# A two-layer encoder in split float32: six weight tiles between the layers get their low parts by accumulating DMA instead of GpSimd subtraction

## The chip, the cores and the metric

The kernel runs on one core of a Trainium2 chip. The metric is the device time of one execution in microseconds (us). The core's engines are named as the profile names them: PE is TensorE's matmul, PEld its weight load, DVE is VectorE, ACT is ScalarE, POOL is GpSimd, SP is SyncE. Engines run in parallel, each its own instructions in order, and wait for one another by semaphores. DMA transfers are issued by the queues of SP, ACT and POOL and run on 16 DMA engines.

## The reference

Two layers (`DEPTH = 2`) work on a float32 stream of 512 tokens by 1024 channels. Each is:

```
h    = rms_norm(x, g_pre_mix);  proj = h @ w_in          # 1024 x 5632
o_a, o_b, o_m = 2-D neighbourhood attention (6 heads, bias from a table rpb_na),
                dilated windows with ALiBi (6 heads), cross-attention to 256 memory tokens
merged = sum of sigmoid(gates) * (o @ w_br)               # three branches
x = x + rms_norm(merged @ w_out, g_post_mix)
u = depthwise_conv(rms_norm(x, g_pre_ffn) @ w_up);  a, b = split(u)
x = x + rms_norm((gelu(a) * b) @ w_down, g_post_ffn)
```

The memory tokens' keys and values are `rms_norm(mem) @ w_mem_kv`, with weights of their own in each layer. The output is `x` after the second layer.

## The kernel before, in words

**Split operands.** All is held transposed: channels on the 128 partitions, tokens along the free axis. Each float32 operand of a matmul is split in two: a high part `hi` in the matmul's own format (float32r) and a low part `lo`, the source less `hi`. A product is three matmuls (`mm3`): hi by hi, hi by lo, and last the weight's `lo` by the other side's `hi`.

**Weights.** `weights` (L227) brings one weight tile of 1024 x 128 (512 KB) by SP's queue into a raw buffer `wraw`, of which there are three. With a `slot` given, it is then split in two chunks of 128 partitions x 512 numbers, each into a buffer of the pool `m` (32 buffers). `split` (L223) copies a chunk to `hi` on ACT, and forms `lo` as `wraw - hi` on VectorE or on GpSimd, as its last argument says. Both read `wraw`, and SP loads the next tile into it when both are done.

**Between the layers.** At the end of layer 0 the new `x` comes in two halves of 256 tokens. For each, a chain on VectorE and ACT normalises and adds (`y<-y,pt`, `x<-x,y`) and sums squares (`acc<-acc,sq`); PE turns the sum into a column (`pt<-mean,acc`), ACT and DVE make the root's reciprocal. Beside this chain PE runs work of layer 1 in an order laid down when the program is built (a planner with a clock of estimated costs, class `Woven`; it is the same order on PE before and after the change):

- `mem_kv`: four tiles of `w_mem_kv`, called kv0 to kv3 here, by the normalised memory tokens.
- `run_group`, first half of tokens: six tiles of `w_in`, called gw0 to gw5, in pairs. A pair takes turns over the eight 128-row pieces k = 0 to 7 of the weights; pieces 0 to 3 lie in a tile's first chunk, 4 to 7 in its second. Pair gw0, gw1 goes into two `mm` banks, pair gw2, gw3 into `o` and `pt`, pair gw4, gw5 into two `s` banks.
- `run_group`, second half, by the not yet normalised `ka` tiles of `raw_end_job`; then a factor `R` scales it, which the second chain yields.

**Who splits which tile.** The strings `KVE` (L38) and `GEN` (L38) say it by one letter for each tile: V is VectorE, G is GpSimd. G has kv2, kv3, gw0, gw1, gw3 and gw5: six tiles, twelve chunks. Their `lo` are first read by PE's third matmul for piece 0 or 4.

**What else POOL does there.** It copies halves of memory keys, and builds layer 1's bias tiles in `a_bias` (L593): a transfer of the table (`y<-in_rpb_dram`, 128 KB, on POOL's queue) into a buffer `y` that the second chain's `x<-x,y` must have read, then three subtractions `y<-mask,y`.

Of the kernel before, what the change touches and what calls it, by code (L numbers as in the profile page):

```python
# [10 lines left out]
ALU = mybir.AluOpType  # L11
# [9 lines left out]
KD = D_MODEL // 128  # L21
# [6 lines left out]
FIRST = (0, 3, 4, 7, 6, 1)  # L28
# [6 lines left out]

LAT_QK, LAT_SM, LAT_T, LAT_V, LAT_T2 = 1.0, 4.5, 1.5, 2.0, 0.6
STEP_A, STEP_B, STEP_M = 9.0, 9.0, 5.5
SQG, LOG, GEN, KVE = {0: (), 1: ()}, {0: (), 1: ()}, 'GGVGVG', 'VVGG'  # L38
SD1 = 4.0
MARGIN = 0.3  # L40
SB = True
# [1 line left out]
KVD, GWD, NG, LAT1 = 7.3, 1.0, 2, 12.0  # L43
# [76 lines left out]
def tile_hybrid_encoder(ctx, tc, xT, memT, memg, vecs, rpb, w_in, w_kv, w_bra, w_brb, w_brm,  # L120
                        w_out, w_up, w_down, c_ident, c_mask, c_tab0, c_tab1, out):
    nc = tc.nc
# [13 lines left out]
    uid, last_copy, last_act, crit, last_lo = [0], [None], [None], [None], {}  # L136
    wv = Woven(tc)

    def nm(s):
        uid[0] += 1  # L140
        return f"{s}_{uid[0]}"


    def big(dt=F32R, shape=(128, 512)):
        return mp.tile(list(shape), dt, tag="m", name=nm("m"))
# [28 lines left out]
    def f32(ap):  # L174
        return ap.bitcast(F32)

    G = nc.gpsimd
    ACT, V = Counted(nc.scalar, wv, 0.1, 0.8e-3), Counted(nc.vector, wv, 0.065, 1.05e-3)

    DUP, MDUP = G, G  # L180
    MSQ = G

    def ready(least):
# [34 lines left out]
    def behind(ins, other):  # L218

        if other is not None and ins is not other:  # L220
            tc.add_manual_dep(ins, other.name, ORDER, reason="issue order")

    def split(src, hi, lo, eng=None):  # L223
        last_copy[0] = ACT.copy(hi, src).ins
        last_lo[eng or V] = (eng or V).tensor_sub(lo, src, f32(hi)).ins

    def weights(src, K, C, slot=None, eng=None, after=None):  # L227

        raw = wp.tile([128, K, C], F32, tag="wraw", name=nm("wraw"))
        nc.sync.dma_start(out=raw, in_=src)  # L230
        if slot is None:
            hi = wp.tile([128, K, C], F32R, tag="whi", name=nm("whi"), bufs=2)
            lo = wp.tile([128, K, C], F32R, tag="wlo", name=nm("wlo"), bufs=2)
            split(raw, hi, lo, eng)
            behind(last_copy[0], after)
            return [(hi[:, k, :], lo[:, k, :]) for k in range(K)]
        n = 512 // C
        w = []
        for k in range(0, K, n):
            c = min(n, K - k)  # L240
            hi, lo = slot(F32R, (128, c, C)), slot(F32R, (128, c, C))
            split(raw[:, k:k + c, :], hi, lo, eng)
            w += [(hi[:, i, :], lo[:, i, :]) for i in range(c)]
        return w

# [68 lines left out]
    def sumsq_add(acc, src, first, slot=None, eng=None):  # L314
        if first:
            ACT.activation(acc, src, AF.Square)
        else:
            n = acc.shape[-1]
            sq = slot((128, 256)) if slot else small("sq2", 4) if n == 256 else small("sq", 1, (128, 512))
            ACT.activation(sq, src, AF.Square)  # L320
            (eng or V).tensor_add(acc, acc, sq)
# [34 lines left out]
    def rtile():  # L356
        return tp.tile([128, 512], F32, tag="R", name=nm("R"), bufs=1)
# [6 lines left out]
    def pre_norm_job(l, goff, acc, hs, i):  # L364
        half, box = HALVES[i], []
        yield from rstd_job(acc if isinstance(acc, list) else [acc[:, half]], 256, box)
        for k in range(KD):
            g = g0[:, k:k + 1] if l == 0 and goff == V_PRE else vec[:, l, goff + k:goff + k + 1]
            normed(xh(k, half), g, box[0], hs[k][0][:, half], hs[k][1][:, half],
                   G if k in LOG[l > 0 and goff == V_PRE] else V)  # L370
        crit[0] = last_copy[0]
        yield 1.2
        wv.give(f"h{l}.{goff}.{i}")
# [73 lines left out]
    def h_tiles():  # L447
        return [(htile(), htile()) for _ in range(KD)]


    def mem_norm_job(l, hm, slot):
        raws = []
        for k2 in range(KD // 2):
            t = slot(F32, (128, 2, N_MEM))
            nc.scalar.dma_start(out=t, in_=memT[:, 2 * k2:2 * k2 + 2, :])
            raws += [t[:, 0, :], t[:, 1, :]]
        acc = small("h32", 3)
        for k in range(KD):
            sumsq_add(acc, raws[k], k == 0, None, MSQ if l else V)
        yield 14.0  # L460
        box = []
        yield from rstd_job([acc], N_MEM, box)
        for k in range(KD):
            t = slot(F32R, (128, 2, N_MEM))
            normed(raws[k], mg[:, k:k + 1], box[0], t[:, 0, :], t[:, 1, :])
            hm.append((t[:, 0, :], t[:, 1, :]))
        yield 1.2
        wv.give(f"mem{l}")
# [10 lines left out]
    def mem_kv(l, hm, km, vm, pre=()):  # L479
        wv.need(f"mem{l}")  # L480
        for m in range(4):
            w = pre[m] if pre else weights(w_kv[l, m], KD, 128)
            ps = mmbank((128, N_MEM))
            linear(ps, w, hm, slice(0, N_MEM))
            if m < 2:
                t, u = big(F32R, (128, 2, N_MEM)), big(F32R, (128, 2, N_MEM))
                twice_split(ps, (t[:, 0, :], t[:, 1, :]), (u[:, 0, :], u[:, 1, :]), None, MDUP)
                km.append((t, u))
            else:
                vT = big(F32, (128, 256))  # L490
                ACT.copy(vT, ps)
                wv.spawn(mem_v_job(l, vT, vm))


    def group_weights(srcs, engs):
        return [weights(s, KD, 128, big, e) for s, e in zip(srcs, engs)]
# [19 lines left out]
    def proj(l, m, hs, after=None):  # L516
        w = weights(w_in[l, m], KD, 128, after=after)
        ps = mmbank()
        linear(ps, w, hs)
        return ps  # L520
# [366 lines left out]
    gw = group_weights([w_in[0, m] for m in FIRST[:2]], (V, V))  # L887
# [14 lines left out]
    for l in range(depth):  # L902
# [41 lines left out]
        for m in range(KD):  # L944
# [3 lines left out]
            hi, lo = big(), big()  # L948
# [4 lines left out]
        hs, R, gw = h_tiles(), rtile(), []  # L953
# [44 lines left out]
        if l == depth - 1:  # L998
            sublayer_end(l, V_POSTF, w_of, fs, 2, None)
            while wv.jobs:  # L1000
                wv._step()
        else:
            hm, km, vm = [], [], []
            wv.spawn(mem_norm_job(l + 1, hm, htile), 20.0)
            pre, R, raw, box = [], rtile(), [], []

            def then(a, i, l=l, box=box):
                box.extend(h_tiles())
                return pre_norm_job(l + 1, V_PRE, a, box, i)

            gw = []

            def kv_ahead(l=l, pre=pre, gw=gw):
                pre.append(weights(w_kv[l + 1, 0], KD, 128, htile))
                yield KVD
                for i in (1, 2, 3):
                    yield 0.9
                    pre.append(weights(w_kv[l + 1, i], KD, 128, big, G if KVE[i] == 'G' else V))
                wv.give(f"kv{l + 1}")
                for m in range(NG):  # L1020
                    yield GWD
                    gw.extend(group_weights([w_in[l + 1, FIRST[m]]], [G if GEN[m] == 'G' else V]))
                wv.give(f"gw{l + 1}")

            sublayer_end(l, V_POSTF, w_of, fs, 1, [then, (box, raw, R)], (1.4, LAT1), lambda: wv.spawn(kv_ahead()))
            wv.need(f"kv{l + 1}")
            mem_kv(l + 1, hm, km, vm, pre)
            wv.need(f"gw{l + 1}")
            gw += group_weights([w_in[l + 1, m] for m in FIRST[NG:]], [G if e == 'G' else V for e in GEN[NG:]])
            wv.need(f"h{l + 1}.{V_PRE}.0")  # L1030
            hs = box

# [92 lines left out]
```

## Time and profile before

| | us |
|---|---|
| median of 3 runs | 1551.7 |
| the three runs | 1549.61, 1551.7, 2167.76 |
| profiled execution | 1551.73 |
| its span, first to last instruction | 1550.0 |
| PE busy | 1522.5 (98%) |
| DVE busy | 951.6 (61%) |
| ACT busy | 712.7 (46%) |
| POOL busy | 149.7 (10%), 217 instructions |

The profiled execution's time is its span and 1.73 us around it. The busy shares are means over the whole span; the change touches some 50 us of it, about 766 to 815 us from its start, and that stretch is to be read by itself.

### The profile page before, as it was taken

What the parts mean: (1) busy time and instruction counts of PE and PEld (TensorE: products, weight loads), DVE (VectorE), ACT (ScalarE), POOL (GpSimd) and SP (SyncE); (2) the same over time, 40 slices, a digit from 0 to 9 for tenths busy, and PEclk for the clock granted to TensorE, in tenths of its full rate; (3) what the DMA queues carried; (4) which work ended last, traced back from release to release, by engine and by line L of the source; (5) the groups of instructions that cost most, each with busy time, mean ns of one, the idle gap of its engine ahead of it and who ended that gap; (6) DMA issues with size and microseconds to landing.
All of it is one profiled execution on the core that took longest, in us unless ns stands there. A gap on an engine that the chain in (4) does not pass through costs nothing.

```text
span 1550.0 us, 20648 instructions
## 1 busy us (share of the span) xinstructions
PE 1522.5 (98%) x7970; PEld 1300.1 (84%) x7970; DVE 951.6 (61%) x1684; ACT 712.7 (46%) x1266; POOL 149.7 (10%) x217
## 2 busy tenths in 40 slices
PE   8999999999999999999989999999999999999997
PEld 7988888888988888888888888888889888888887
DVE  6685676335777777742497756753456977776233
ACT  5565554336544444532355555532354544444231
POOL 3340000110000000000154300002100000000000
PEclk9999999999999999999999999999999999999999
DMA  7221213235113322333431221132350233323331
GB/s 246 89 88 64 62 57 107 84 95 165 53 59 100 100 96 95 118 90 101 129 102 59 78 66 58 61 104 88 102 177 15 82 96 99 101 99 89 99 105 63
DMA packets 45810, 144.91 MB, mean 93 GB/s; under 512 B 5376, under 2 KB 9600, under 8 KB 45712
## 3 DMA queue, kind: packets, MB, share of 16 engines
q1 hardware_dynamic: 43776, 139.85, 28.5%
q10 hardware_dynamic: 1296, 2.10, 0.4%
q0 software_dynamic: 640, 1.64, 0.3%
q8 instruction: 62, 1.02, 0.3%
q14 instruction: 36, 0.29, 0.1%
HBM read 141.48 MB, written 2.10 MB: 93 GB/s over the span
## 4 chain that ended last, share of the span: by engine, by line
PE 91%; DVE 6%; ACT 2%; issue 1%; DMA 0%; SPq 0%; ACTq 0%; DVEq 0%
PE mm L247 80%; PE s L247 4%; PE o L247 3%; PE pt L258 2%; DVE m L114 1%; DVE y L114 1%; PE pt L247 1%; DVE ka L114 1%; DVE x L114 1%; ACT y L114 1%; DVE st L114 0%; DVE acc L114 0%; DMA x<-in_xT_dram 0%; DVE wlo L114 0%; ACT whi L114 0%
## 5 line engine op out<-in xcount | busy, mean ns | idle before, releaser
L247 PE MATMUL mm<-h,whi 128*128 128x512 f32 x2496 | 776.5, 392 | 0.0
L247 PEld LDWEIGHTS mm<-h,whi 128*128 128x128 f32 x2496 | 462.0, 188 | 91.3
L247 PE MATMUL mm<-h,wlo 128*128 128x512 f32 x1248 | 486.9, 390 | 0.0
L114 DVE TENSOR_TENSOR wlo<-wraw,whi 128x1024 fp32r<-128x1024 f32 (+1 forms) x213 | 259.2, 1217 | 284.7 <-ACT whi L114 282.3
L114 ACT CAST whi<-wraw 128x1024 fp32r<-128x1024 f32 (+1 forms) x213 | 221.4, 1040 | 307.8 <-PE mm L247 293.4
L247 PEld LDWEIGHTS mm<-h,wlo 128*128 128x128 f32 x1248 | 234.5, 188 | 49.6
L247 PE MATMUL mm<-m,whi 128*128 128x512 f32 (+1 forms) x800 | 215.1, 356 | 1.0 <-DVE m L114 0.8
L247 PEld LDWEIGHTS mm<-m,whi 128*128 128x128 f32 x800 | 141.8, 189 | 22.8 <-PE mm L247 1.3
L247 PE MATMUL mm<-m,wlo 128*128 128x512 f32 (+1 forms) x400 | 142.1, 355 | 0.0
L114 DVE SCALAR_TENSOR_TENSOR y<-y,vec,y 128x511 f32<-128x511 f32 x176 | 130.5, 748 | 3.5 <-ACT y L114 0.9
L114 DVE TENSOR_TENSOR y<-mm,R 128x512 f32<-128x512 f32 x82 | 56.4, 688 | 68.5 <-PE mm L247 68.5
L247 PEld LDWEIGHTS mm<-m,wlo 128*128 128x128 f32 x400 | 75.5, 189 | 10.9
L802 POOL TENSOR_TENSOR m<-m,y 128x512 f32<-128x512 f32 x28 | 36.1, 1289 | 399.4 <-DVE y L114 399.4
L114 ACT ACTIVATE y<-y,vec 128x512 f32<-128x512 f32 x88 | 71.1, 815 | 2.3 <-DVE y L114 1.9
L247 PE MATMUL mm<-m,m 128*128 128x512 f32 x240 | 63.5, 394 | 0.0
L114 ACT ACTIVATE y<-y 128x512 f32<-128x512 f32 x44 | 27.9, 633 | 71.7 <-DVE y L114 71.3
L114 ACT CAST m<-pt 128x512 fp32r<-128x512 f32 (+1 forms) x72 | 38.6, 541 | 46.8 <-PE pt L258 38.5
L114 ACT ACTIVATE y<-y,st 128x256 f32<-128x256 f32 (+1 forms) x80 | 43.8, 549 | 30.4 <-DVE st L114 28.9
L114 DVE TENSOR_TENSOR acc<-acc,sq 128x256 f32<-128x256 f32 (+1 forms) x80 | 41.1, 514 | 26.6 <-ACT sq L114 24.7
L114 DVE TENSOR_TENSOR m<-pt,m 128x512 fp32r<-128x512 f32 (+1 forms) x72 | 45.1, 630 | 19.9 <-ACT m L114 18.6
L114 ACT CAST m<-y 128x512 fp32r<-128x512 f32 x32 | 19.9, 622 | 72.5 <-DVE y L114 72.5
L247 PE MATMUL mm<-h,m 128*128 128x256 f32 x312 | 49.1, 301 | 2.0 <-ACT h L114 1.0
(154 smaller groups left out, 1789.9 us busy)
## 6 DMA issues: line engine op xcount, KB each, us to landing
wraw<-in_w_in_dram SPq DMA_DIRECT2D x88, 512.0 KB, 3.7
wraw<-in_w_up_dram SPq DMA_DIRECT2D x88, 512.0 KB, 3.6
wraw<-in_w_down_dram SPq DMA_DIRECT2D x32, 512.0 KB, 3.5
wraw<-in_w_out_dram SPq DMA_DIRECT2D x16, 512.0 KB, 3.9
wraw<-in_w_down_dram SPq DMA_DIRECT2D x16, 384.0 KB, 3.1
wraw<-in_w_kv_dram SPq DMA_DIRECT2D x8, 512.0 KB, 4.0
wraw<-in_w_bra_dram SPq DMA_DIRECT2D x16, 192.0 KB, 2.3
x<-in_xT_dram SPq DMA_DIRECT2D x8, 256.0 KB, 7.3
```

The source lines that it names most:

```text
L114: return op(*args, **kw)
L247: wv.pe(nc.tensor.matmul(ps, a, b, start=first, stop=last), cost)
L258: wv.pe(nc.tensor.transpose(ps[:, 128 * i:128 * i + 128], s, ident), 0.11)
L802: (V if br == 2 and m >= 6 else G).tensor_add(acc[m], acc[m], gs)
```

## The change

In six tiles the letter G becomes D. For a D tile ACT still copies the chunk to `hi`. GpSimd then writes `-hi` into `lo`, one instruction with one input, and issues a DMA that reads the same chunk of the weights from memory once more and adds it onto `lo` where it lies. `lo` is again the weight less `hi`. `wraw` is now read by ACT alone. The two G tiles of layer 0's first group stay as they were.

```diff
--- before.py
+++ after.py
@@ -35,7 +35,7 @@
 
 LAT_QK, LAT_SM, LAT_T, LAT_V, LAT_T2 = 1.0, 4.5, 1.5, 2.0, 0.6
 STEP_A, STEP_B, STEP_M = 9.0, 9.0, 5.5
-SQG, LOG, GEN, KVE = {0: (), 1: ()}, {0: (), 1: ()}, 'GGVGVG', 'VVGG'
+SQG, LOG, GEN, KVE = {0: (), 1: ()}, {0: (), 1: ()}, 'DDVDVD', 'VVDD'
 SD1 = 4.0
 MARGIN = 0.3
 SB = True
@@ -178,6 +178,7 @@
     ACT, V = Counted(nc.scalar, wv, 0.1, 0.8e-3), Counted(nc.vector, wv, 0.065, 1.05e-3)
 
     DUP, MDUP = G, G
+    ENG = {'G': G, 'V': V, 'D': 'D'}
     MSQ = G
 
     def ready(least):
@@ -239,7 +240,12 @@
         for k in range(0, K, n):
             c = min(n, K - k)
             hi, lo = slot(F32R, (128, c, C)), slot(F32R, (128, c, C))
-            split(raw[:, k:k + c, :], hi, lo, eng)
+            if eng == "D":
+                last_copy[0] = ACT.copy(hi, raw[:, k:k + c, :]).ins
+                nc.gpsimd.tensor_scalar_mul(lo, f32(hi), -1.0)
+                nc.gpsimd.dma_start(out=lo, in_=src[:, k:k + c, :], accum_op=ALU.add)
+            else:
+                split(raw[:, k:k + c, :], hi, lo, eng)
             w += [(hi[:, i, :], lo[:, i, :]) for i in range(c)]
         return w
 
@@ -1015,18 +1021,18 @@
                 yield KVD
                 for i in (1, 2, 3):
                     yield 0.9
-                    pre.append(weights(w_kv[l + 1, i], KD, 128, big, G if KVE[i] == 'G' else V))
+                    pre.append(weights(w_kv[l + 1, i], KD, 128, big, ENG[KVE[i]]))
                 wv.give(f"kv{l + 1}")
                 for m in range(NG):
                     yield GWD
-                    gw.extend(group_weights([w_in[l + 1, FIRST[m]]], [G if GEN[m] == 'G' else V]))
+                    gw.extend(group_weights([w_in[l + 1, FIRST[m]]], [ENG[GEN[m]]]))
                 wv.give(f"gw{l + 1}")
 
             sublayer_end(l, V_POSTF, w_of, fs, 1, [then, (box, raw, R)], (1.4, LAT1), lambda: wv.spawn(kv_ahead()))
             wv.need(f"kv{l + 1}")
             mem_kv(l + 1, hm, km, vm, pre)
             wv.need(f"gw{l + 1}")
-            gw += group_weights([w_in[l + 1, m] for m in FIRST[NG:]], [G if e == 'G' else V for e in GEN[NG:]])
+            gw += group_weights([w_in[l + 1, m] for m in FIRST[NG:]], [ENG[e] for e in GEN[NG:]])
             wv.need(f"h{l + 1}.{V_PRE}.0")
             hs = box
```

The scheduler that lays out each engine's instructions moves some of them. On POOL, from the second of the two places where its D chunks stand (gw3 and gw5; `m` are the `lo` and `hi` chunks, `in_rpb_dram` the bias table), before:

```order
L225 TENSOR_TENSOR m_7245<-wraw_7242,m_7244 128x512
L225 TENSOR_TENSOR m_7249<-wraw_7242,m_7248 128x512
L225 TENSOR_TENSOR m_7265<-wraw_7262,m_7264 128x512
L225 TENSOR_TENSOR m_7269<-wraw_7262,m_7268 128x512
L596 DMA y_7760<-in_rpb_dram 128x256
L599 TENSOR_TENSOR y_7759<-mask,y_7760 128x256 x2
L599 TENSOR_TENSOR y_7760<-mask,y_7760 128x256
```

and now:

```order
L245 TENSOR_SCALAR m_7253<-m_7252 128x512
L246 DMA m_7253<-in_w_in_dram 128x512
L245 TENSOR_SCALAR m_7258<-m_7257 128x512
L602 DMA y_7772<-in_rpb_dram 128x256
L246 DMA m_7258<-in_w_in_dram 128x512
L245 TENSOR_SCALAR m_7275<-m_7274 128x512
L605 TENSOR_TENSOR y_7771<-mask,y_7772 128x256
L246 DMA m_7275<-in_w_in_dram 128x512
L245 TENSOR_SCALAR m_7280<-m_7279 128x512
L605 TENSOR_TENSOR y_7771<-mask,y_7772 128x256
L246 DMA m_7280<-in_w_in_dram 128x512
L605 TENSOR_TENSOR y_7772<-mask,y_7772 128x256
```

The table's transfer and two of the three subtractions that wait for its landing now stand between the weights' own transfers. At the first place (kv2, kv3, gw0, gw1) eight subtractions become eight pairs of `TENSOR_SCALAR` and `DMA`, with nothing between them.

On VectorE, at the start of the second chain (`wraw` and `m` are gw4's chunks, whose `lo` VectorE forms; `y` and `x` are the chain), before:

```order
L114 TENSOR_TENSOR y_6072<-y_6072,pt_7304 128x256
L114 TENSOR_TENSOR y_6073<-y_6073,pt_7304 128x256
L114 TENSOR_TENSOR m_7255<-wraw_7252,m_7254 128x512
L114 TENSOR_TENSOR x<-x,y_6072 128x256
L114 TENSOR_TENSOR m_7259<-wraw_7252,m_7258 128x512
L114 TENSOR_TENSOR x<-x,y_6073 128x256
L114 SCALAR_TENSOR_TENSOR ka_7296<-x,vec,ka_7296 128x256
L114 TENSOR_TENSOR y_6074<-y_6074,pt_7304 128x256
```

and now:

```order
L114 TENSOR_TENSOR y_6072<-y_6072,pt_7316 128x256
L114 TENSOR_TENSOR y_6073<-y_6073,pt_7316 128x256
L114 TENSOR_TENSOR x<-x,y_6072 128x256
L114 TENSOR_TENSOR x<-x,y_6073 128x256
L114 TENSOR_TENSOR y_6074<-y_6074,pt_7316 128x256
L114 TENSOR_TENSOR m_7265<-wraw_7262,m_7264 128x512
L114 SCALAR_TENSOR_TENSOR ka_7308<-x,vec,ka_7308 128x256
L114 TENSOR_TENSOR m_7269<-wraw_7262,m_7268 128x512
L114 SCALAR_TENSOR_TENSOR ka_7309<-x,vec,ka_7309 128x256
```

Both of gw4's subtractions now come behind the first two additions to `x`.

## Rows read from the trace of the kernel before

**Rows 1.** Page, chain that ended last: shares of the span by engine.

```profile
PE 91%; DVE 6%; ACT 2%; issue 1%; DMA 0%; SPq 0%; ACTq 0%; DVEq 0%
```

**Rows 2.** Timeline of TensorE, 740 to 830 us: start, duration, instruction, count [idle before <-releaser].

```profile
783.59 0.58 PE L247 MATMUL pt<-mean,acc 128*128 128x1 f32 x4 [3.46 <-DVE acc L114]
...
786.10 4.79 PE L247 MATMUL mm<-h,m 128*128 128x256 f32 x30
...
795.72 3.12 PE L247 MATMUL mm<-h,m 128*128 128x256 f32 x24
...
799.04 0.52 PE L247 MATMUL pt<-h,m 128*128 128x256 f32 x3
...
804.44 5.92 PE L247 MATMUL s<-h,m 128*128 128x256 f32 x48
...
813.64 0.58 PE L247 MATMUL pt<-mean,acc 128*128 128x1 f32 x4 [1.16 <-DVE acc L114]
```

**Rows 3.** Stretches: length, busy time of PE, PEld, DVE, ACT, POOL, PEclk, DMA, GB/s.

```profile
785.00:788.00 3.00, 2.90 (x15) 2.61 (x14) 2.57 (x8) 1.44 (x5) 2.13 (x6) 0.50 0.03 5
790.00:794.00 4.00, 4.00 (x36) 4.00 (x35) 3.73 (x11) 2.98 (x9) 0.00 (x0) 1.00 0.00 0
```

**Rows 4.** Timeline of GpSimd (POOL), 700 to 920 us.

```profile
768.30 6.93 POOL L225 TENSOR_TENSOR m<-wraw,m 128x512 fp32r<-128x512 f32 x5 [105.56 <-ACT m L114]
776.61 4.24 POOL L225 TENSOR_TENSOR m<-wraw,m 128x512 fp32r<-128x512 f32 x3 [1.39 <-ACT m L114]
...
795.61 2.99 POOL L225 TENSOR_TENSOR m<-wraw,m 128x512 fp32r<-128x512 f32 x2 [8.35 <-PE s L258]
800.96 2.92 POOL L225 TENSOR_TENSOR m<-wraw,m 128x512 fp32r<-128x512 f32 x2 [2.36 <-ACT m L114]
```

**Rows 5.** Groups on POOL, 700 to 920 us: count, busy us, mean ns.

```profile
L225 POOL TENSOR_TENSOR m<-wraw,m 128x512 fp32r<-128x512 f32 x12 | 17.1, 1452 | 117.7 <-ACT m L114 109.3 <-PE s L258 8.4
```

**Rows 6.** Groups on VectorE (DVE), 769 to 784 us.

```profile
L114 DVE TENSOR_TENSOR x<-x,y 128x256 f32<-128x256 f32 x8 | 6.7, 868 | 0.0
L114 DVE TENSOR_TENSOR acc<-acc,sq 128x256 f32<-128x256 f32 x8 | 5.1, 648 | 0.3 <-ACT sq L114 0.2
L114 DVE TENSOR_TENSOR y<-y,pt 128x256 f32<-128x256 f32 x8 | 3.0, 410 | 0.9 <-PE pt L342 0.9
```

**Rows 7.** Groups on DVE, 794.6 to 814 us.

```profile
L114 DVE TENSOR_TENSOR x<-x,y 128x256 f32<-128x256 f32 x8 | 4.8, 608 | 0.0
L114 DVE TENSOR_TENSOR acc<-acc,sq 128x256 f32<-128x256 f32 x7 | 4.0, 566 | 0.4
```

**Rows 8.** VectorE instructions on tile x, whole span: duration min/median/max ns.

```profile
L114 DVE TENSOR_TENSOR x<-x,y x60: 410/419/1517, 402.0 to 1545.6; 128x256 f32<-128x256 f32 x60
```

**Rows 9.** Groups on POOL, whole span.

```profile
L293 POOL CAST ka<-ka 64x512 fp32r<-64x512 f32 x12 | 7.5, 627 | 42.6 <-ACT ka L114 42.1
```

**Rows 10.** POOL instructions on tile y, 700 to 1000 us: min/median/max ns; landing in us.

```profile
L599 POOL TENSOR_TENSOR y<-mask,y x18: 720/736/1722, 808.2 to 882.4; 128x256 f32<-128x256 f32 x18
L596 POOL DMA_DIRECT2D y<-in_rpb_dram x6: 556/556/556, 803.8 to 876.7; - x6
...
DMA to landing us min/median/max: 2.3/2.8/4.2
```

**Rows 11.** DMA issues: queue, count, KB each, median us from issue to landing.

```profile
wraw<-in_w_in_dram SPq DMA_DIRECT2D x88, 512.0 KB, 3.7
...
wraw<-in_w_brm_dram SPq DMA_DIRECT2D x8, 256.0 KB, 2.7
...
vec<-in_vecs_dram SPq DMA_DIRECT2D x1, 232.0 KB, 7.8
```

**Rows 12.** Timeline of ScalarE (ACT), 794.5 to 795.5 us.

```profile
794.87 1.13 ACT L114 CAST m<-wraw 128x512 fp32r<-128x512 f32 x2
```

**Rows 13.** Timeline of DVE, 799.3 to 799.7 us.

```profile
798.81 0.68 DVE L114 TENSOR_TENSOR m<-wraw,m 128x512 fp32r<-128x512 f32 x1
799.41 0.41 DVE L114 TENSOR_TENSOR x<-x,y 128x256 f32<-128x256 f32 x1
```

## The prediction

> **What bounds the kernel now.** I read the chain of waits first: 91% of the span is PE [rows 1], so almost everywhere only PE's own work counts, and work moved on POOL is free. The exception is the stretch that the change touches. PE's timeline shows it standing still twice there: 3.46 us before 783.59 and 1.16 us before 813.64, both times for `acc`, the end of a VectorE chain [rows 2]. After the first gap PE's granted clock is 0.50 (the 1.2 GHz level) from 785 to 788, and 1.00 (2.4 GHz) from 790 on [rows 3]; after the 1.16 us gap PE's rows run on at full pace. 30 matmuls took 4.79 us at the low clock, where 24 like them took 3.12 [rows 2]: 30 x 0.130 = 3.9, so 0.9 us lost.
>
> Why is VectorE late? In that stretch GpSimd forms low parts, eight from 768.30 to 780.85 and four between 795.61 and 803.88 [rows 4], 1.452 us each [rows 5]. While it does, additions with two SBUF inputs take long: `x<-x,y` 0.868 us and `acc` 0.648 in the mean [rows 6], against a median of 0.419 over the program for the same shape [rows 8]. `y<-y,pt`, which has one input in PSUM, stays at 0.410 [rows 6]. The excess is 8 x 0.449 + 8 x 0.229 = 5.4 us in the first chain; in the second, x 8 x 0.189 + acc 7 x 0.147 = 2.5 [rows 7].
>
> The Trainium skill (SBUF — State Buffer, section "Who interferes with whom") says that a VectorE instruction with two SBUF inputs and a GpSimd instruction that reads SBUF exclude one another, and whichever starts first holds for its whole length. The rows agree (0.868 against 0.410); by that rule the new multiplication still excludes VectorE, only for less long.
>
> **The change part by part.** The profiled execution, 1551.73 us, is the base; the median of the runs is 1551.7, the same.
>
> *POOL.* Twelve subtractions go (12 x 1.452 = 17.4 us). Twelve multiplications by -1 come; none is in the trace. Bounds are a copy of as many numbers per partition, 0.627 [rows 9], and the subtraction, 1.452; I take 0.7, near the copy, since both have one input. Twelve issues come, 0.556 each as for the bias table, shortest and longest alike [rows 10]. 12 x 1.256 = 15.1 us: POOL is no busier.
>
> *The landing.* The low part is ready only when its transfer has landed. I call that time, from issue, L. No accumulating transfer is in the trace. The bias table on the same queue, 128 KB, took 2.3 to 4.2 us, median 2.8 [rows 10]; on SP's queue 256 KB take 2.7 and 512 KB 3.7 [rows 11], so 0.5 us for each further 128 KB. 256 KB on POOL's queue: 3.3. Adding must also read the target; counted as 256 KB more, 4.3. I take 4.3; the ends are 2.3 (the fastest table) and 7.8 (a 232 KB transfer at the program's busy start) [rows 11].
>
> The Trainium skill (DMA: Bandwidth & Descriptors, section "Anatomy of one DMA — SWDGE (gpsimd) path") has a fit of 2.0 us plus bytes over 436 GB/s, by which 256 KB would be an estimated 2.6. The rows' 128 KB at 2.8 lie above that fit's 2.3, so the rows decide; with 2.6 the sum below would come to -3.1.
>
> *First place (kv2, kv3, gw0, gw1).* A multiplication plus an issue (1.26) is shorter than a subtraction, so the last issue ends no later than 780.85 and lands 3.7 us on, 784.6. The new order puts ACT's copies of gw1 behind two more squares, some 2 us: 786.6. The 48 matmuls of pair gw0, gw1 end at 798.84 [rows 2], so at 0.130 each they begin at 792.6 and read the second chunks' lows 3 us later. Covered, also when PE is 3.7 us early, by 2 us or more; past that cover each us would be PE's. What is won here is collisions: 5.4 x (1 - 0.7/1.452) = 2.8 us off the chain. PE's gap shrinks from 3.46 to 0.7, shorter than the gap of 1.16 that cost no clock, so the 0.9 comes back too: PE 3.7 us early, the VectorE and ACT chain 2.8.
>
> *Second place (gw3, gw5), where it is given back.* ACT's copy of gw3's first chunk ends at 795.4 (two in 1.13 from 794.87 [rows 12]), now 792.6; multiplied 793.3; landed 797.6. PE wants it as the third matmul of the row at 799.04 [rows 2], 799.3, now 795.6: **PE waits 2.0 us**, where it waited for nothing. Behind the multiplication of the second chunk POOL now waits for VectorE: the table's transfer, ahead of the weights' in the queue, needs a `y` buffer that `x<-x,y` frees. That one ended at 799.82 [rows 13]; it moves by 2.8 and by the two subtractions put behind it (2 x 0.68), to 795.6. The table is issued, then at 796.2 the chunk: landed 800.5. PE wants it 24 matmuls (3.1 us) after 797.6, 800.7: just in time.
>
> gw5's first transfer stands behind a `y<-mask,y`, which waits for the table. With 4.2, the longest landing, since weights load beside it, that is 799.8, plus 0.736 for the subtraction [rows 10]: issued 800.5, landed 804.8. PE wants it at the sixth matmul after 804.44 [rows 2], 5.8 us after gw3's: 803.4. **PE waits 1.4 us.** Its second chunk: issued at 802.5, landed 806.8, wanted 807.9: no wait.
>
> *The sum.* PE came to the end of this work at 813.64 - 1.16 = 812.48, 13.2 us after gw3's first low. Now: 797.6 + 13.2 + 1.4 = 812.2. The second VectorE chain ends at 813.64 - 2.8 - 1.3 (half of its 2.5) = 809.5, so `acc` no longer holds PE. 812.2 against 813.64: **-1.4 us**, 1550.3. The wait of 2.0 is nearer to 1.16 than to 3.46; I count no lower clock for it (0.9 if it comes). Everything after follows PE and moves along. SP's loads of `wraw` are released by ACT alone, up to 2 us sooner; no load is waited for there, so nothing is counted. The chunks read twice add 12 x 256 KB, 3 MB in some 35 us, priced in L alone.
>
> Ends. L = 2.3, the table's too: no wait is left, PE comes at 812.48 - 3.7 = 808.8, the chain at 809.5: -4.1. L = 7.8: 801.1 + 13.2 + 0.9 (a long wait lowers the clock) + 0.5 at gw5 = 815.7: +2.1. If the collisions all went as well as L = 2.3, PE is 3.46 + 0.9 early and waits nowhere: 808.1, -5.5. If all stayed, gw3's first low lands at 800.4, 1.1 late, and gw5's at 807.7 by the same steps, wanted at 806.2: 800.4 + 13.2 + 1.5 = 815.1, +1.5; with L = 7.8 too, 803.9 + 13.2 + 0.9 + 0.6 = 818.6, +5.0. So 1546.2 to 1556.7.
>
> **The rivals.**
>
> *The low parts come in time.* L near 3, or the multiplication collides less than its length: both gaps vanish and no new one comes. -3 to -5.5, 1546.2 to 1548.7. For it: the fastest table's 2.3. Against: the table's transfer and subtraction now stand in the queue before gw5.
>
> *Slower: the wait moves to gw3.* Collisions stay (the multiplication reads SBUF too) or L is 6 to 8, and PE waits for gw3's first low longer than it gained: +1 to +5, 1552.7 to 1556.7. It decides at about L = 5.7, where the -1.4 is used up. The change would then not do what it says, take GpSimd out of VectorE's way. For it: nothing in the trace shows an adding transfer. Against: the copy's 0.627.
>
> *Slower: POOL's issue is long.* If an issue took q instead of 0.556, POOL itself would bind: 768.3 + 12 x (0.7 + q) + 2.1 for the table + 3.7 for landing + 4.3 of PE's work behind gw5's last chunk = 786.8 + 12q. That passes 813.64 at q = 2.2, costs 9 us at 3, and 31 us (2%) at 4.8. Against it: six issues of 0.556 beside a busy VectorE.
>
> The Trainium skill (SBUF — State Buffer, section "SBUF: two separate sides") warns that VectorE in a two-port mode keeps GpSimd from writing a transfer's descriptors, which would lengthen q. The six equal issues give no sign of it here.
>
> **How the numbers follow.** Forecast (1548.7 to 1552.7): 50 in 100. In time: 20. Wait at gw3: 20. Long issue: 10, of it 3 beyond 31 us. The likeliest time is 1550.3. The range 1546 to 1558 takes in the first three with their ends and the runs' own 2 us of scatter, and leaves out most of the long issue. About 2%, 31 us, is what a measurement of this kernel can tell from no change; no case reaches 1520. So faster 0.01, same 0.96, slower 0.03.
>
> **What the new profile would show.** `TENSOR_SCALAR` on POOL near 0.7 us; `x<-x,y` in the first chain near 0.65 instead of 0.868; PE's gap before the first `pt<-mean,acc` under 1.2 us and full clock behind it; a new PE wait for a DMA at `pt<-h,m`, and a smaller one in the `s` group; no wait at the second `pt<-mean,acc`. I am wrong if L is under 3 or over 6, if an issue takes over 1 us, or if VectorE's additions stay at 0.868.

## The result, and the profile after

The change made the kernel slightly slower: 1554.88 us in the median of 22 runs against 1551.36 for the kernel before on the same chip, a ratio of 1.0022 [1.0016, 1.0028], +3.5 us. The forecast was -1.4. The profiled execution took 1555.72 us, against 1551.73. One run of each kernel, of 2167.76 us before and 3085.0 us now, was far slower than the rest and is left out of the ratio.

All of the loss lies in the stretch that the prediction looked at. From the first `pt<-mean,acc` of the first chain to the one before `R`, the kernel before took 45.83 us (767.81 to 813.64), the changed one 50.02 (769.02 to 819.04): +4.2. Its stretch begins 1.21 us later, in work that the change does not touch, so 1.21 is to be taken off its clock times when they are held against those of [rows 2].

The shares of the chain of waits, which answer to [rows 1]:

```profile
PE 92%; DVE 4%; ACT 1%; DMA 1%; issue 1%; POOL 0%; SPq 0%; ACTq 0%; POOLq 0%
```

DMA, at 0% before, has 1%. TensorE's timeline of the changed kernel shows where (start, duration, instruction, count [idle before <-releaser]):

```profile
783.59 0.58 PE L253 MATMUL pt<-mean,acc 128*128 128x1 f32 x4 [2.25 <-DVE acc L114]
786.04 0.69 PE L348 MATMUL pt<-ident,st 128*128 128x128 f32 x2 [0.70 <-DVE st L114]
786.38 4.95 PE L253 MATMUL mm<-h,m 128*128 128x256 f32 x30
...
802.77 0.58 PE L253 MATMUL pt<-h,m 128*128 128x256 f32 x1 [2.23 <-DMA m<-in_w_in_dram]
803.15 0.84 PE L253 MATMUL o<-h,m 128*128 128x256 f32 x3
803.79 0.84 PE L253 MATMUL pt<-h,m 128*128 128x256 f32 x3
...
808.78 0.39 PE L253 MATMUL pt<-h,m 128*128 128x256 f32 x1 [1.48 <-DMA m<-in_w_in_dram]
...
811.15 5.92 PE L253 MATMUL s<-h,m 128*128 128x256 f32 x48
...
819.04 0.50 PE L253 MATMUL pt<-mean,acc 128*128 128x1 f32 x4
```

Against [rows 2], the first gap shrank by only 1.21 us, from 3.46 to 2.25, and a wait of 0.70 follows it. Two new waits stand in pair gw2, gw3, both for the accumulating transfers: 2.23 us for gw3's first chunk and 1.48 for its second. The `s` group waits for nothing, and neither does the last `pt<-mean,acc`, which had waited 1.16: TensorE arrives there so late that the VectorE chain is done.

Stretches of the same trace (length, then busy time of PE, PEld, DVE, ACT, POOL, then PEclk, DMA share, GB/s):

```profile
784.00:788.00 4.00, 3.30 (x20) 3.10 (x20) 3.14 (x10) 1.94 (x6) 3.41 (x4) 0.68 0.98 217
790.00:794.00 4.00, 4.00 (x36) 4.00 (x35) 3.75 (x11) 3.03 (x9) 3.53 (x7) 1.00 0.75 121
...
800.00:804.00 4.00, 1.77 (x10) 1.57 (x9) 4.00 (x8) 2.28 (x6) 3.72 (x4) 0.82 0.99 222
804.00:808.00 4.00, 3.30 (x20) 3.10 (x19) 4.00 (x9) 1.76 (x5) 2.71 (x3) 0.76 0.94 273
```

The granted clock falls after both long waits, the second time where [rows 2] had none: groups of three matmuls follow one another at 0.64 us from 803.15, and at 0.36 once the clock is back. The DMA engines are 0.94 to 0.99 busy in the three stretches at the waits; before, they were 0.03 busy from 785 to 788 [rows 3] and 0.63 from 800 to 804.

POOL's timeline, first where its chunks follow one another, then at gw3:

```profile
776.93 0.90 POOL L246 DMA_DIRECT2D m<-in_w_kv_dram  x1 [0.30 <-DVE y L114]
777.55 1.83 POOL L245 TENSOR_SCALAR m<-m 128x512 fp32r<-128x512 f32 x1
779.68 0.90 POOL L246 DMA_DIRECT2D m<-in_w_kv_dram  x1 [0.30 <-DVE x L114]
780.30 1.82 POOL L245 TENSOR_SCALAR m<-m 128x512 fp32r<-128x512 f32 x1
...
795.38 0.59 POOL L300 CAST m<-m 64x256 fp32r<-64x256 f32 x1
796.09 1.78 POOL L245 TENSOR_SCALAR m<-m 128x512 fp32r<-128x512 f32 x1
798.16 0.91 POOL L246 DMA_DIRECT2D m<-in_w_in_dram  x1 [0.30 <-POOL m L245]
798.80 1.82 POOL L245 TENSOR_SCALAR m<-m 128x512 fp32r<-128x512 f32 x1
800.25 0.91 POOL L602 DMA_DIRECT2D y<-in_rpb_dram  x1
800.92 1.15 POOL L246 DMA_DIRECT2D m<-in_w_in_dram  x1
```

A chunk takes 2.75 us here (777.55 to 780.30), against 1.45 for a subtraction [rows 4, 5] and the 1.26 predicted. These rows overlap: the issue of 776.93 ends at 777.83, the multiplication's row begins 0.28 before that, and from there to its end at 779.38 are 1.55 us. So the 2.75 are 1.55 for the multiplication, 0.30 of idle time and 0.90 for the issue. Before each issue POOL idles 0.30 us for its own multiplication; where the row names VectorE as releaser, that one had long been done. At gw3 everything stands in line: multiplied from 796.09, issued at 798.16, landed for 802.77. The groups by source line (duration min/median/max ns, first and last start) and the landing of all twelve:

```profile
L245 POOL TENSOR_SCALAR m<-m x12: 1557/1826/2217, 769.5 to 806.8; 128x512 fp32r<-128x512 f32 x12
...
L246 POOL DMA_DIRECT2D m<-in_w_in_dram x8: 891/903/1229, 782.4 to 808.9; - x8
...
DMA to landing us min/median/max: 3.8/5.0/7.8
```

VectorE's groups from 769 to 784 us, which answer to [rows 6]:

```profile
L114 DVE TENSOR_TENSOR x<-x,y 128x256 f32<-128x256 f32 x8 | 7.1, 901 | 0.0
L114 DVE TENSOR_TENSOR acc<-acc,sq 128x256 f32<-128x256 f32 x8 | 4.1, 521 | 0.2 <-ACT sq L114 0.2
L114 DVE TENSOR_TENSOR y<-y,pt 128x256 f32<-128x256 f32 x8 | 3.0, 410 | 0.9 <-PE pt L348 0.9
```

`x<-x,y` got no faster (0.868 before), `acc` a little (0.648). GpSimd holds VectorE nearly as much as it did.

### The profile page after: what moved, and what is told of

It reads as the page before. It is cut to its first block, busy times and chain, and to the rows that moved or that the text cites. A ratio compares the mean times of both kernels' runs of the same rounds, so it can differ in the third digit from the quotient of the medians.

```text
span 1554.0 us, 20681 instructions
## 1 busy us (share of the span) xinstructions
PE 1521.9 (98%) x7970; PEld 1300.2 (84%) x7970; DVE 954.3 (61%) x1684; ACT 710.8 (46%) x1266; POOL 163.9 (11%) x229
## 4 chain that ended last, share of the span: by engine, by line
PE 92%; DVE 4%; ACT 1%; DMA 1%; issue 1%; POOL 0%; SPq 0%; ACTq 0%; POOLq 0%
PE mm L253 80%; PE s L253 5%; PE o L253 4%; PE pt L264 2%; PE pt L253 1%; DVE y L114 1%; DVE m L114 1%; DMA m<-in_w_in_dram 1%; DMA x<-in_xT_dram 0%; DVE ka L114 0%; DVE x L114 0%; ACT whi L114 0%; ACT y L114 0%; DVE wlo L114 0%; DVE h L114 0%
## 5 line engine op out<-in xcount | busy, mean ns | idle before, releaser
L114 DVE TENSOR_TENSOR m<-wraw,m 128x512 fp32r<-128x512 f32 (+1 forms) x58 | 38.1, 669 | 22.2 <-ACT m L114 22.2
```

Source lines behind the costliest of these rows:

```text
L114: return op(*args, **kw)
```

## Experiments

One theory from the two traces: **A**, the low part of gw3 is late because POOL's own steps are long and the transfer comes on top; what is lost is lost at the second place. Rivals, which the expectations call B to D as they bring them in: GpSimd's collisions with VectorE, the traffic beside the weights' loads, the adding itself; and the bias table in the queue. A second question is why the collisions stayed. The table gathers the twelve kernels; the stretch is that defined above, each from one profiled execution (the changed kernel: 50.02, the kernel before: 45.83). Waits of TensorE for other things, each under 0.9 us, are left out of the last column. Every ratio is against the kernel before on the same chip (1550.2 to 1550.9).

| kernel | median us | ratio | stretch | TensorE's waits for acc, DMA, POOL |
|---|---|---|---|---|
| first place alone | 1550.60 | 0.9999 [0.9990, 1.0009] | 46.01 | 2.27 acc, 0.93 acc |
| second place alone | 1553.89 | 1.0031 [1.0019, 1.0042] | 49.73 | 3.44 acc; 2.10, 1.27 DMA |
| ScalarE writes -hi | 1551.22 | 1.0004 [0.9993, 1.0014] | 46.61 | 1.58, 2.22, 1.57 DMA |
| table behind the weights | 1552.88 | 1.0020 [1.0010, 1.0030] | 49.65 | 2.27 acc; 2.44, 1.00 DMA |
| copy for multiplication | 1552.12 | 1.0009 [1.0000, 1.0018] | 48.21 | 2.51 acc; 2.93 DMA |
| multiplication alone | 1543.73 | 0.9959 [0.9946, 0.9971] | 39.85 | 0.23 acc |
| transfer without adding | 1551.66 | 1.0009 [1.0000, 1.0018] | 48.55 | 1.15 acc; 1.53, 2.83 DMA |
| ScalarE, first place alone | 1547.43 | 0.9980 [0.9971, 0.9989] | 42.96 | 0.46 acc, 0.88 DMA, 1.24 acc |
| the same, gw3 and gw5 on VectorE | 1549.34 | 0.9990 [0.9980, 0.9999] | 42.56 | 1.47 DMA, 1.66 acc |
| all six tiles on VectorE | 1547.27 | 0.9977 [0.9968, 0.9986] | 42.43 | 1.96 acc |
| two multiplications, two transfers | 1557.21 | 1.0040 [1.0028, 1.0052] | 52.82 | 1.49 acc; 1.21, 5.40, 1.66 DMA |
| traffic from SyncE | 1549.75 | 0.9988 [0.9978, 0.9997] | 45.36 | 3.60 POOL |

### One place at a time

```diff
-SQG, LOG, GEN, KVE = ..., 'DDVDVD', 'VVDD'
+SQG, LOG, GEN, KVE = ..., 'DDVGVG', 'VVDD'   # first place alone
+SQG, LOG, GEN, KVE = ..., 'GGVDVD', 'VVGG'   # second place alone
```

> The accumulating transfers only for kv2, kv3, gw0 and gw1; gw3 and gw5 by GpSimd subtraction as before. Theory A (the loss is at gw3: PE waits there for landings, 2.23 and 1.48 us, and runs at the low clock after): 1551 to 1552, within 1 us of the kernel before. Theory B (a multiplication of 1.83 us shuts VectorE out as long as the subtraction of 1.45 did, so the chains are no shorter and POOL is late everywhere): 1553 to 1554.5, two thirds of the loss stay. Theory C (the transfers crowd out the weight loads, which land 1.5 to 3 us later): 1553 to 1554.

> The accumulating transfers only for gw3 and gw5; the other four tiles by GpSimd subtraction as before. Theory A: all of the loss, 1554.5 to 1556, with PE waits at pt<-h,m of 2 us and more. Theory B: a third of the loss, 1552 to 1553. Theory C: 1552 to 1553.

The first place alone costs nothing and gains nothing; `x<-x,y` of the first chain stays at 0.903 there. The second alone costs 3.7 us (1553.89 against 1550.17), about the whole loss, with two waits for transfers as in the changed kernel:

```profile
782.62 0.58 PE L253 MATMUL pt<-mean,acc 128*128 128x1 f32 x4 [3.44 <-DVE acc L114]
800.43 0.45 PE L253 MATMUL pt<-h,m 128*128 128x256 f32 x1 [2.10 <-DMA m<-in_w_in_dram]
806.34 0.39 PE L253 MATMUL pt<-h,m 128*128 128x256 f32 x1 [1.27 <-DMA m<-in_w_in_dram]
```

There is no backlog from the first place here, and the first wait is still 2.10: the steps of one chunk are enough to make it late. This bears theory A out.

### POOL's part of the steps

ScalarE writes -hi at both places, so that POOL only issues:

```diff
-                nc.gpsimd.tensor_scalar_mul(lo, f32(hi), -1.0)
+                ACT.activation(lo, raw[:, k:k + c, :], AF.Copy, scale=-1.0)
```

> The negative high part is written by ScalarE from the raw tile, with the scale -1, instead of a GpSimd multiplication; the transfers stay. Theory A: POOL issues at once, gw3's first low part lands about 2 us sooner, so most of the wait at gw3 goes: 1550 to 1552.5. Theory B: the collisions go as well (x<-x,y back at 0.42 us in the first chain, PE's gap of 2.25 us before the first pt<-mean,acc gone): 1549 to 1551. Theory C: 1553.5 to 1555, since every transfer is still there.

A copy in place of the multiplication (the low part is then `hi` plus the weight, so the output is not the reference's):

```diff
-                nc.gpsimd.tensor_scalar_mul(lo, f32(hi), -1.0)
+                nc.gpsimd.tensor_copy(lo, f32(hi))
```

> GpSimd copies the high part into the low buffer instead of multiplying it by -1; the transfer then adds the weight onto it (the low part is then the weight plus its high part, so the output is not the reference's). Theory A (the multiplication at 1.83 us, priced at 0.7, is what fails): the copy takes 0.6 us, PE's first gap shrinks below 1 us, gw3's first low lands 1.2 us sooner after its high part, and the time comes near the forecast of -1.4 us: 1549 to 1550.5 where the kernel before is at 1550.2. Theory D (the adding transfers carry only some 256 KB per 2.4 us and queue up behind one another once POOL issues them faster): landings grow to 7 us and more, waits at gw1, gw3 and gw5, and the time stays at 1551 to 1552.5.

With ScalarE's -hi the first gap is gone, the stretch is 3.4 us shorter than the changed kernel's (46.61 against 50.02), and the time is again that of the kernel before. The wait at gw3, of which theory A expected most to go, is still 2.22: its chunk is issued sooner, and TensorE comes sooner too. With one wait for gw1 (1.58) and one for gw5 (1.57) there are three, all for transfers, whose landings are now the long term:

```profile
L246 POOL DMA_DIRECT2D m<-in_w_in_dram x8: 866/875/1205, 773.2 to 802.5; - x8
...
DMA to landing us min/median/max: 4.1/8.0/11.3
```

Issued sooner, the eight of the first place take longer and longer to land: 6.9 us from its issue for the first, 11.3 for the sixth, 10.5 for the eighth.

The copy takes 0.61 to 0.73 us where no issue stood right ahead of it. Its row reads 0.93 where one did, but overlaps the issue's as above:

```profile
769.82 0.88 POOL L246 DMA_DIRECT2D m<-in_w_kv_dram  x1 [0.30 <-DVE x L114]
770.38 0.93 POOL L245 CAST m<-m 128x512 fp32r<-128x512 f32 x1
```

From the issue's end at 770.70 to its own at 771.31 are 0.61 us. The copy shortens the stretch by 1.8. Theory A's first gap under 1 us did not come (2.51), gw3's first low part is still waited for (2.93), and the time, 1552.12, is not near the forecast but where theory D had it, though without that theory's waits at gw1 and gw5.

### The queue, and the adding

The table's transfer put behind the weights' own at gw3:

```diff
-                nc.gpsimd.dma_start(out=lo, in_=src[:, k:k + c, :], accum_op=ALU.add)
+                last_lo[G] = nc.gpsimd.dma_start(out=lo, in_=src[:, k:k + c, :], accum_op=ALU.add).ins
```

> The bias table's transfer is ordered behind the last accumulating transfer, as it was behind the last subtraction before. Theory A: gw3's second chunk, which landed 7.8 us after its issue with the table's transfer ahead of it, lands about 3 us sooner, and the 1.48 us wait goes: 1553 to 1554. Theory B: no change, 1554 to 1555.5. Theory C: a little, 1554.

The transfer without adding (the low part is then the weight itself, and the output not the reference's):

```diff
-                nc.gpsimd.dma_start(out=lo, in_=src[:, k:k + c, :], accum_op=ALU.add)
+                nc.gpsimd.dma_start(out=lo, in_=src[:, k:k + c, :])
```

> The same transfers without the addition: they write the weight over the negative high part (so the output is not the reference's). Theory D (adding costs the DMA engines about double): landings fall from 5.0 us in the median to 3.5, gw3's second chunk from 7.8 to about 5, the wraw loads back to 4: 1551 to 1552.5. Theory A: the multiplication and the issue still stand before each landing, about 1 us better than the changed kernel, 1552.5 to 1553.5. If adding costs nothing, no difference: 1553.5 to 1554.

The table matters little: without it ahead, gw3's second chunk still lands 7.4 us after its issue, the second wait falls from 1.48 to 1.00 only, and the stretch by 0.4. The plain transfer gives 1.5 us of the stretch back, but not at gw3, where the two waits are 1.53 and 2.83 against 2.23 and 1.48. It comes from the first chain: the gap there is 1.15 instead of 2.25, and the 30 matmuls behind it take 3.84 us instead of 4.95, without a low clock. Its issue and landing:

```profile
L246 POOL DMA_DIRECT2D m<-in_w_in_dram x8: 535/576/598, 779.3 to 804.6; - x8
...
DMA to landing us min/median/max: 2.8/3.9/6.6
```

So adding costs 0.33 us at the issue (0.903 against 0.576) and 1.1 in the median landing. On the DMA engines it costs more. POOL's queue (q0) and SP's (q1) from 765 to 825 us (packets, MB, share of the time of 16 engines), in the changed kernel:

```profile
q0 software_dynamic: 1824, 3.41, 33.1%
q1 hardware_dynamic: 1405, 5.10, 25.7%
```

and with plain transfers:

```profile
q1 hardware_dynamic: 1298, 4.72, 22.4%
q0 software_dynamic: 1824, 3.41, 19.4%
```

Over 60 us, 3.41 MB took 33.1% with adding, 5.8 us of all engines per MB, and 19.4% without, 3.4, near SP's 3.0 and 2.8. Loads of `wraw` in the stretch landed in 5.2 us in the median, against 3.7 before [rows 11].

### Multiplication, issue and traffic apart

The multiplication alone (the low part stays -hi, so the output is not the reference's):

```diff
-                nc.gpsimd.dma_start(out=lo, in_=src[:, k:k + c, :], accum_op=ALU.add)
```

> The multiplication alone, without the transfer: the low part stays the negative high part (so the output is not the reference's). Theories A and D: no landing, so no wait at gw3; x<-x,y stays at 0.9 us in the first chain: 1550 to 1551, the time of the kernel before. Theory B (the multiplications' collisions with VectorE make the loss): 1552 to 1553.5, most of the loss stays.

The second reading issued by SyncE and brought into `wraw`:

```diff
-                nc.gpsimd.dma_start(out=lo, in_=src[:, k:k + c, :], accum_op=ALU.add)
+                nc.sync.dma_start(out=raw[:, k:k + c, :], in_=src[:, k:k + c, :])
```

> As the changed kernel's multiplications by GpSimd, but the second reading of each chunk is issued by SyncE and lands, without adding, in wraw again, which nothing reads afterwards: the low part is left at -hi, so the output is not the reference's, and no engine waits for these transfers. It keeps the twelve 256 KB of traffic beside the multiplications and takes away GpSimd's issues. Theory, that the issues on GpSimd are what lengthens the multiplications and holds VectorE: multiplications 1.48 to 1.52 back to back, x<-x,y of the first chain 0.42, no wait before the first pt<-mean,acc; 1543 to 1546, as with the multiplications alone, up to 2 us more if the weights' loads behind the added transfers come late. Rival, that the transfers' traffic into SBUF does it: multiplications near 1.8, x near 0.9, and 1548 to 1552.

Both multiplications of a tile ahead of both transfers:

```diff
-                nc.gpsimd.tensor_scalar_mul(lo, f32(hi), -1.0)
-                nc.gpsimd.dma_start(out=lo, in_=src[:, k:k + c, :], accum_op=ALU.add)
+                neg = nc.gpsimd.tensor_scalar_mul(lo, f32(hi), -1.0).ins
+                los.append((lo, src[:, k:k + c, :]))
...
+        for lo, part_src in los:
+            behind(nc.gpsimd.dma_start(out=lo, in_=part_src, accum_op=ALU.add).ins, neg)
```

> As the changed kernel, but both multiplications of a tile come before both of its transfers, so that only every other multiplication stands right behind an issue. Theory B, that what stands right behind an issue of GpSimd's is 0.33 us longer and holds VectorE: first multiplication of a pair 1.8, second 1.50; x<-x,y of the first chain between the 0.42 without transfers and the 0.90 with them, near 0.65. Rival, that it is the landing traffic of the transfers: every multiplication 1.8 and x 0.90 again. By both, gw3's first low part is multiplied at the same time and issued 1.5 us later, so PE's wait there grows from 2.2 to 3 to 4 us, less what the chain gains: 1554 to 1557, ratio 1.002 to 1.004.

The multiplication alone shows two things. Its own price is 1.50 us, twice what was predicted, and it hardly holds VectorE. POOL's timeline and VectorE's groups of the first chain, in that kernel:

```profile
766.10 11.93 POOL L245 TENSOR_SCALAR m<-m 128x512 fp32r<-128x512 f32 x8 [105.58 <-ACT m L114]
```

```profile
L114 DVE TENSOR_TENSOR x<-x,y 128x256 f32<-128x256 f32 x8 | 3.1, 415 | 0.0
L114 DVE TENSOR_TENSOR acc<-acc,sq 128x256 f32<-128x256 f32 x8 | 4.0, 506 | 1.1 <-ACT sq L114 0.9
```

Eight multiplications stand back to back from 766.10 to 778.03, beside eight additions to `x` with two SBUF inputs at 0.415. Only `acc` is a little longer, 8 x 0.087 = 0.7 us above 0.419 in all, against the 5.4 of the subtractions. With the traffic added by SyncE it is the same:

```profile
L245 POOL TENSOR_SCALAR m<-m x12: 1480/1490/1760, 767.0 to 802.9; 128x512 fp32r<-128x512 f32 x12
```

```profile
L114 DVE TENSOR_TENSOR x<-x,y 128x256 f32<-128x256 f32 x8 | 3.1, 413 | 0.0
```

So the traffic is not what holds VectorE. (That kernel's time, expected at 1543 to 1546, came to 1549.75: POOL's new order put three of the bias table's subtractions, begun only at 798.23, ahead of gw5's multiplications, and TensorE waited 3.60 us for the first.) Nor are the issues alone: with ScalarE's -hi eight of them lie beside the first chain, and `x<-x,y` is 0.416. VectorE is held where a GpSimd instruction follows an issue of GpSimd's: `x<-x,y` is 0.901 in the changed kernel, 0.763 with plain transfers, so the adding is not needed for it. In the changed kernel one such addition reads:

```profile
777.29 1.50 DVE L114 TENSOR_TENSOR x<-x,y 128x256 f32<-128x256 f32 x1
```

It begins while the issue of 776.93 runs, and ends in the multiplication of 777.55 that follows. How issue and multiplication join is not settled. The pairs were to tell whether only the instruction right behind an issue suffers. The rows of their multiplications are long, 2.17 and 1.88 us in the second pair, 2.44 and 2.55 in the third, which neither theory foresaw, but they overlap with what stands ahead of them. The third pair:

```profile
776.24 2.23 POOL L251 DMA_DIRECT2D m<-in_w_kv_dram  x2
777.56 4.01 POOL L245 TENSOR_SCALAR m<-m 128x512 fp32r<-128x512 f32 x2
```

From the end of the two issues, 778.47, to the end of the two multiplications, 781.57, are 3.10 us, 1.55 each. So the issues ahead do not lengthen a multiplication, here or in the changed kernel, and the expected 0.33 us was overlap. What issues and multiplications together do is hold VectorE: `x<-x,y` came to 0.742, between 0.42 and 0.90 as the first theory had it. The later issue cost more than was expected, 5.40 us of waiting at gw3 instead of 3 to 4, and the time, 1557.21, lies at the upper end of what was expected.

The Trainium skill (SBUF — State Buffer, section "Who interferes with whom") says that a transfer has ports of its own and never contends with a compute engine, and the trace with SyncE's traffic agrees (0.413). The same section's rule that a VectorE instruction with two SBUF inputs contends with a GpSimd instruction that reads SBUF holds here for the subtraction (0.868 [rows 6]), and hardly for the multiplication alone (0.415, and `acc` 0.506); the measurement decides.

### Versions that beat both

ScalarE's -hi at the first place and GpSimd's subtraction for gw3 and gw5; then VectorE for those two; then VectorE for all six, without transfers:

```diff
-                nc.gpsimd.tensor_scalar_mul(lo, f32(hi), -1.0)
+                ACT.activation(lo, raw[:, k:k + c, :], AF.Copy, scale=-1.0)
-SQG, LOG, GEN, KVE = ..., 'DDVDVD', 'VVDD'
+SQG, LOG, GEN, KVE = ..., 'DDVGVG', 'VVDD'   # first
+SQG, LOG, GEN, KVE = ..., 'DDVVVV', 'VVDD'   # second
+SQG, LOG, GEN, KVE = ..., 'VVVVVV', 'VVVV'   # third, ScalarE's line not reached
```

> ScalarE writes the negative high part, and the accumulating transfers serve kv2, kv3, gw0 and gw1 only; gw3 and gw5 by GpSimd subtraction as before. Theories A and D: the first chain runs without collisions (x<-x,y 0.42 us), PE is 3 to 5 us early at the second place and waits for no landing there; the second chain of VectorE becomes the bound: 1547 to 1549, 1.5 to 3 us faster than the kernel before. Theory B: the same gain or more. Theory C (crowded weight loads): a wait at gw1 or gw2 eats it, 1550 to 1551.

> As the kernel with ScalarE writing -hi and transfers at the first place only, but gw3 and gw5 split by VectorE, so that GpSimd forms no low part in the stretch. Theory: that kernel's second VectorE chain still had about 2.8 us of collisions with four GpSimd subtractions (one x<-x,y of 1.51, one ka of 1.51); four VectorE subtractions cost 4 x 0.60 = 2.4 instead. So the end moves by only -0.4: ratio to before 0.997 to 0.998, 1546.5 to 1547.5, and the last wait for acc stays near 1.2 us. Rival, that what GpSimd leaves is worth its whole collision while VectorE has room for four subtractions: last wait gone, 1545 to 1546. Rival, that the first VectorE subtractions ahead of the chain hold it: +1, 1548 to 1549.

> No transfers at all: VectorE forms the low parts of the six tiles. Theory: the collisions of the kernel before (5.4 us in the first chain, 2.5 in the second) go, and 12 subtractions of 0.60 us pitch come, 4.8 us beside the first chain and 2.4 in the second: nothing won, 1550 to 1552, ratio 0.999 to 1.001. If instead the subtractions fit into VectorE's idle time in the first chain (it waits 3 us there for ScalarE's squares), 1547 to 1549, ratio 0.997 to 0.998, and transfers are not needed for the gain that they give with ScalarE's -hi.

The first and the third beat both kernels, by 3.4 and 3.5 us against the kernel before, and the third reads nothing twice. Its VectorE groups from 765 to 784 us:

```profile
L114 DVE TENSOR_TENSOR m<-wraw,m 128x512 fp32r<-128x512 f32 x10 | 6.6, 688 | 0.8 <-ACT m L114 0.8
...
L114 DVE TENSOR_TENSOR x<-x,y 128x256 f32<-128x256 f32 x8 | 3.1, 419 | 0.0
```

No GpSimd instruction lies beside the first chain, the additions are at their 0.419, and the subtractions fit in between: the first gap is gone. The second version's stretch is the 0.4 us shorter that was expected (42.56 against 42.96), but its median is 1.9 longer. Its profiled execution is longer behind the stretch, in work that all these kernels share: 738.0 us, where the other profiles have 734.2 to 737.2. Why is open.

## Why the prediction was wrong

The forecast was a gain of 1.4 us, and the kernel lost 3.5. The step that failed is the way of gw3's first low part: the multiplication was priced at 0.7 us and took 1.55 (at gw3's first chunk 1.78), and the collisions that were to bring everything forward by 2.8 us stayed. The time, 1554.9, lies within the range by the second rival alone (wait at gw3: +1 to +5), which had 20 in 100 where the forecast had 50. Its reason, that the multiplication reads SBUF too, is not what the multiplication alone shows. Of the named signs of being wrong, VectorE's additions staying at 0.868 came true.

- **The multiplication was mis-sized.** The step "I take 0.7, near the copy, since both have one input" failed: 1.55 us from the end of the issue ahead (its row says 1.83), and 1.50 without transfers, above the subtraction's 1.452 that was its upper bound. A row of before would have warned, the only multiplication by a number that GpSimd did there:

```profile
L890 POOL TENSOR_SCALAR hb<-vec 128x48 f32<-128x48 f32 x1 | 0.3, 336 | 8.5 <-DMA vec<-in_vecs_dram 8.5
```

48 numbers took 0.336 us, copies of 8 numbers 0.18 to 0.26: some 2 to 4 ns for each further number, so an estimated 1.2 to 2.1 for 512.

- **"What is won here is collisions", 2.8 us, failed.** Excess in the first chain is now 8 x 0.482 + 8 x 0.102 = 4.7 us, against 5.4: 0.7 won. The reason given was wrong as well: the multiplication hardly holds VectorE by itself, but does together with GpSimd's issues.
- **The issue** was put at 0.556 and took 0.90, with 0.30 idle ahead of it (longer rows, up to 1.23, overlap with the row ahead). The row it was read from is of a transfer that does not add; plain, the weights' issue is 0.576. With the multiplication that is 2.75 us for a chunk, 33 for twelve, so "POOL is no busier" failed too. It was not the third rival's q (it needed 2.2).
- **The landing**: 5.0 in the median for 4.3 predicted, 4.6 for gw3's first chunk and 7.8 for its second. For the first chunk L was nearly right and TensorE waited all the same, so "it decides at about L = 5.7" failed too: that point assumed the other terms.
- **The sum.** On the clock of before, gw3's first low part was there at 802.77 - 1.21 = 801.56, predicted 797.6: 4.0 late. ScalarE's copy ended at 795.95 - 1.21 = 794.74 instead of 792.6 (2.1, for the collisions that stayed; GpSimd, idle for 8.35 us ahead of gw3 before [rows 4], was itself busy until 795.97); from there to the issue 798.16 - 795.95 = 2.2 instead of 0.7 (1.5); landing 0.3. From it to the last `pt<-mean,acc` TensorE took 16.27 us, where 13.2 + 1.4 were predicted: the 1.4 came, as 1.48 at gw3's second chunk instead of at gw5, and 1.6 on top, 1.25 of it the low clock (four times a pitch of 0.64 for 0.36, once 0.49), which was counted at nothing. 4.0 + 0.1 + 1.6 = 5.7, about the difference between -1.4 and +4.2.
- **Right were** the place, a new wait at `pt<-h,m` for a DMA, and that the first place is covered (the first place alone: no wait for a transfer, 1550.6). It is not covered "also when PE is 3.7 us early": with ScalarE's -hi TensorE ends the first chain 3.6 us earlier against the stretch's start and waits 1.58 for gw1.
- **Right by luck** was that the last `pt<-mean,acc` would not wait. The second VectorE chain was to end at 809.5 and ended at 816.42 - 1.21 = 815.2, later than before; TensorE came later still:

```profile
812.80 3.62 DVE L114 TENSOR_TENSOR acc<-acc,sq 128x256 f32<-128x256 f32 x6
```

The rival in which the low parts come in time was put at 3 to 5.5 us. Multiplications alone, with no transfer to wait for and `x<-x,y` at 0.415, gained 7.1.

## What to carry to other kernels

A subtraction handed to an accumulating transfer becomes a chain of copy, negation, issue and landing; add it up against the slack of its first reader, there and not over the program: at gw3 it was some 7 us from the end of the copy to the low part (795.95 to 802.77). For a new operation look for the same operation in the trace, however small, before one that only resembles it. Where a row begins before the row ahead of it on its engine has ended, count its time from that end. And where two engines hold each other up, try first to let the one with room do the work alone: VectorE did all twelve chunks for a gain that the transfers reached only with ScalarE's help.

## What the runs showed of the hardware

- Adding in the transfer took the DMA engines 5.8 us per MB against 3.4 without, and landings of 6.9 to 11.3 us where GpSimd issued eight with nothing to do between them (8.5 to 11.8 with ScalarE's -hi at the first place alone).
- GpSimd's multiplication by a number, 128 x 512: 1.50 us alone, and 1.55 from the end of an issue ahead of it; its copy 0.61 both ways. The rows behind an issue read 1.83 to 2.55 and 0.93, because they begin before the row ahead has ended.
- GpSimd's issue of 256 KB: 0.576 plain, 0.87 to 0.90 accumulating.
- VectorE's additions with two SBUF inputs: 0.415 beside back-to-back multiplications on GpSimd, 0.416 beside issues alone; 0.901 beside the two in turn, 0.763 where the transfers do not add.
